# Seven eighths of the output projection planned inside the attention and RWKV stage, with one set of PSUM banks and a bias table written pair by pair

## The chip, the cores and the metric

The kernel runs on one core of a Trainium2 chip, in one launch. The core has a matrix engine (TensorE, PE in the profile, with its weight loads as PEld), two elementwise engines (VectorE, DVE; ScalarE, ACT), a slower general one (GpSimd, POOL) and a queue that issues transfers (SyncE, SP). Each works its own instructions in order, and semaphores hold one back until what it needs is done. The metric is device time in microseconds for one execution, the median of several runs. All times below are microseconds unless marked ns.

## What is computed

One layer over 512 tokens behind 16 meta tokens, width 1024, float32. Two branches of 16 heads read the same normalised input: attention over a window of 128 with a bias table and sinks, and an RWKV-7 recurrence. Gates merge them, an output projection follows, then a normalisation and an MLP. Cut to what matters:

```python
h = layer_norm(concat([meta, x]), ln0_g, ln0_b)          # 528 x 1024
proj = h @ w_in
q, k, v, zr, gate_att, gate_rwkv = split(proj)
att = sliding_window_attention(q, k, v, rel_bias, sinks)
rw = rwkv7_time_mix(zr, ...)                             # token shift, decay, state, group norm
merged = sigmoid(gate_att) * att + sigmoid(gate_rwkv) * rw
h = layer_norm(ALPHA * h + merged @ w_out, ln1_g, ln1_b)
ff = square(relu(h @ w_ff1)) @ w_ff2
out = layer_norm(ALPHA * h + ff, ln2_g, ln2_b)[meta:]
```

## The kernel before

**Products.** Every large product is made of three matmuls in a reduced float32 format: each factor is split in a high and a low part, and high by high, high by low and low by high are added up (`three`). A weight arrives as a raw tile of 128 x 1024 (`wraw`, two of them), ACT casts it to the high part (`whi`), DVE subtracts to get the low part (`wlo`); both are kept in halves of 512 columns. The normalised input lies transposed in `hhi` and `hlo` (128 x 8 x 528), one slice `k` of 128 channels for each of the eight steps of a contraction.

**The stage.** Heads are worked in eight pairs. For each pair `rwkv(j)` makes decay, key, receptance and value from five products, then scores within chunks of 64 tokens, the inverse of a triangular matrix for each chunk, folds, a chain of eight small products (`link`, one for each chunk), outputs, a group norm, and a tile `z`. The inverse goes through memory: blocks `Nd` are stored and gathered as `Nf`, POOL substitutes (`Xf`), the result is stored (`xtd`, `Xrd`) and gathered as `XB`, `X1` (`X` in the profile) and `XTm`. `attention(j)` makes queries, scores with a bias, softmax, the output and both gates. `merge(j)` gates and adds the two into `z` and stores it in DRAM (`md`).

**The order.** None of this is ordered as written. Each function records operations in a plan: `op(engine, cost, fn, r=, w=, new=)`, with an estimated cost, what is read and written, and which buffers are taken (`new`) from rings of tiles (`Ring`, `Buf`). `order` then places all operations by a list schedule at build time: for each engine the ready operation with the earliest due time goes next. Due times are counted back from the end of each pair, `SLOT` (58 us) times its number. A PE operation of another kind than the last (`mode`) is put back by `HYST`. A transfer's result is taken to be there a fixed lag after its issue, 2.3 us or a number beside it. What comes out is a fixed sequence for each engine; on the chip the semaphores wait for the data itself, whatever the plan thought.

**Memory.** PSUM has eight banks: three (`dn`) for the dense products and five (`pg`) for all else. Fourteen tiles (`e`) serve the elementwise work. The bias of the relative distance is made once: a table of 16 heads by 128 values is written to DRAM 128 times over (`tbd`, 1 MB), and each pair reads its part of it along a diagonal (`bias`).

**After the stage.** `merged(j)` loads `md[j]`, halves and splits it into `mhi` and `mlo`. `project_out(k, w, b)` adds slice `k` for block `b` of 128 tokens, both halves of the columns, six products; the first four `k` run over all blocks, the last four block by block. `norm_rows` normalises the input rows again for the residual, `first_norm(b)` adds the projection, normalises, transposes and splits into `h1hi` and `h1lo`; for the first two blocks it is issued between the products of later blocks (`NORMED`). The MLP follows (`up`, `project`), with its first three steps in two halves of tokens.

Of the kernel before, what the change touches and what calls it, by code (L numbers as in the profile page):

```python
# [77 lines left out]
HYST = 4000.0  # L78
# [6 lines left out]
NE = 14  # L85
# [8 lines left out]
SUBST = 1  # L94

# [52 lines left out]
class Buf:  # L148

    def __init__(self, ring):  # L150
# [21 lines left out]
class Plan:  # L172
# [3 lines left out]
    SAFE = SAFE  # L176

# [3 lines left out]
    def op(self, eng, cost, fn, r=(), w=(), new=(), mode="R", lag=None, after=(), part=None, port=0):  # L181
        o = Op(len(self.ops), eng, cost, fn, mode, self.LAG[eng] if lag is None else lag)
        o.part, o.port = part, port
# [29 lines left out]
    def stuck(self, cand, ready):  # L213
        out = []
        for e, c in cand.items():
            for _, o in sorted(c, key=lambda c: c[1].due)[:6]:
                out.append(f"{e} {o.fn.__qualname__.split('<locals>.')[-1]}:{o.fn.__code__.co_firstlineno} due {o.due / 1e3:.0f} new {[(len(b.ring.slots), len(b.ring.bufs), b.turn, b.ring.given) for b in o.new]}")
        held = {}
        for o in self.ops:
            if o.start is not None:  # L220
                for b in o.bufs:
                    if b.first is not None and b.first.start is not None and any(u.start is None for u in b.users):
                        held[b] = 1
        for b in held:
            if len(b.ring.bufs) > 30:
                out.append(f"held of {len(b.ring.bufs)}: {b.first.fn.__code__.co_firstlineno} due {b.first.due/1e3:.0f} left {[u.fn.__code__.co_firstlineno for u in b.users if u.start is None][:4]}")
        return "\n".join(out)

    def order(self, due, hyst, batch=0.0, hold=0.0, begin={}):
        for o in reversed(self.ops):  # L230
# [6 lines left out]
        port = 0.0  # L237
# [5 lines left out]
        wait = {o: len(o.deps) for o in self.ops}  # L243
        cand = {e: [] for e in self.LAG}
        left = {}
        for o in self.ops:
            for b in o.bufs:
                left[b] = len(b.users)
            if not o.deps:
                cand[o.eng].append((0.0, o))  # L250
        done, mode = [], "R"
        rings = {}

        def ready(t, o):
# [3 lines left out]
            for ring, bs in need.items():  # L258
                if len(ring.slots) < len(bs):
                    return None  # L260
                if ring.fifo and min(b.turn for b in bs) != ring.given:
                    return None
# [7 lines left out]
        while len(done) < len(self.ops):  # L270
# [21 lines left out]
            assert best is not None, "no operation can go on: " + self.stuck(cand, ready)  # L292
# [13 lines left out]
            for b in o.new:  # L306
                b.ring.slots.sort(key=lambda s: s[0])
                b.t = b.ring.slots.pop(0)[1]
                b.ring.given += 1
            o.start, o.end = t, t + cost  # L310
            if o.port:
# [7 lines left out]
            for s in o.after:  # L319
                wait[s] -= 1  # L320
                if wait[s] == 0:
                    cand[s.eng].append((max(self.seen(q, s.eng) for q in s.deps), s))
        return sorted(done, key=lambda o: (o.start, o.n))

@with_exitstack
def hybrid_layer_kernel(ctx: ExitStack, tc: tile.TileContext, I: dict, out: bass.AP):
# [4 lines left out]
    pps = ctx.enter_context(ExitStack())  # L331
    dn = pps.enter_context(tc.tile_pool(name="dn", bufs=3, space=PSUM))
    pg = pps.enter_context(tc.tile_pool(name="pg", bufs=5, space=PSUM))
# [51 lines left out]
    vps = pg.tile([P, 512], F32, name="vps", tag="g")  # L385
# [83 lines left out]
    tm = pg.tile([P, 512], F32, name="tm", tag="g")  # L469
# [16 lines left out]
    for k in range(KT):  # L486
        ks = slice(k * P, (k + 1) * P)
        if k % 2 == 0:
            tp = pg.tile([P, 512], F32, name="tp", tag="g")
        else:  # L490
            tp = pg.tile([P, 512], F32, name="tp", tag="g")
# [31 lines left out]
    rest = CONST.shape[1]  # L523
    nc.sync.dma_start(con[:, w0:rest], I["consts"][:, w0:rest])
# [30 lines left out]
    rdn = Ring([dn.tile([P, 512], F32, name="dn", tag="dn") for _ in range(3)], False)  # L555
# [1018 lines left out]
```

## Time and profile before

| | |
|---|---|
| median of 3 runs | 1019.02 us (1018.38 to 1019.12) |
| profiled execution | 1015.6 us, its span from first to last instruction 1013.8 us |
| mean granted PE clock | 0.964 |
| PE busy | 941.1 us |
| DVE, ACT, POOL busy | 578.8, 463.0, 127.8 us |
| transfers | 93.55 MB, mean 92 GB/s |

The profile is of one execution, taken by the hardware profiler. The page gives busy time of each engine, the span in 40 equal slices with busy tenths, and the costliest groups of instructions as `line engine operation out<-in shapes xcount | busy, mean ns | idle before, and what ended it`. Other views used below are: busy time by stretches of time, which ends with the granted clock (1.00 is full), the DMA share and GB/s; waits (who waited for whom: total, times, longest); the chain of work that ended last; and a timeline (start, duration, engine, line, operation, in brackets the idle time before it and what ended it). Durations of matmuls overlap, so distances between starts say more of their rate.

### The profile page before, as it was taken

Reading aid. Unit: us, or ns where it says so; the run is one execution under the profiler, and the core shown is the slowest. Engines: PE = TensorE matmul, PEld = TensorE weight load, DVE = VectorE, ACT = ScalarE, POOL = GpSimd, SP = SyncE. Lnnn points to the kernel's source line nnn. Section 1 sums busy time; section 2 is a strip of 40 time slices with the busy share of each in tenths; the row PEclk is TensorE's granted clock in tenths of the full one; section 3 lists DMA queues with packets and bytes.
Section 4 is the critical chain, followed back from the end, with each engine's and each line's share of the span. In section 5 each row is a group of like instructions: output and inputs, shape, how many; then the busy total and the mean of one; then the engine's idle time right before and its main releaser. Section 6 shows DMA issues by size and latency. Waiting matters only on the chain.

```text
span 1013.8 us, 18375 instructions
## 1 busy us (share of the span) xinstructions
PE 941.1 (93%) x7336; PEld 798.9 (79%) x7336; DVE 578.8 (57%) x1121; ACT 463.0 (46%) x1106; POOL 127.8 (13%) x372
## 2 busy tenths in 40 slices
PE   4996998998999989989999849999999999999996
PEld 3885896887978969879798638798888888888885
DVE  7653575674855847749467538766442334453336
ACT  5652646555565555464654523554431214343120
POOL 2030024041130230401304010000000000000001
PEclk9997999999999989999999959999999999999999
DMA  6345214043151340332403346123332323332232
GB/s 218 124 104 100 69 45 118 28 116 73 44 117 31 96 85 29 102 61 58 101 22 97 83 148 223 53 73 107 123 99 89 104 87 101 103 99 88 83 105 83
DMA packets 83311, 93.55 MB, mean 92 GB/s; under 512 B 54935, under 2 KB 61833, under 8 KB 83225
## 3 DMA queue, kind: packets, MB, share of 16 engines
q1 hardware_dynamic: 81728, 90.29, 32.0%
q10 hardware_dynamic: 1496, 2.08, 0.6%
q8 instruction: 57, 0.93, 0.4%
q14 instruction: 30, 0.24, 0.1%
HBM read 83.10 MB, written 9.26 MB: 91 GB/s over the span
## 4 chain that ended last, share of the span: by engine, by line
PE 63%; DMA 12%; POOL 9%; DVE 8%; issue 3%; ACT 3%; SPq 2%; DVEq 0%; POOLq 0%; ACTq 0%
PE dps L520 6%; PE dps L519 6%; PE dps L521 6%; PE acc L1389 6%; PE acc L1391 6%; PE acc L1390 6%; PE dn L519 4%; POOL ftmp L1015 4%; POOL Xf L1019 4%; PE dn L520 3%; PE dn L521 3%; DMA X<-Xrd 2%; DMA xtd<-Xf 2%; DMA Nd<-NT 2%; DMA Nf<-Nd 2%
## 5 line engine op out<-in xcount | busy, mean ns | idle before, releaser
L519 PE MATMUL dn<-hhi,whi 128*128 128x512 f32 (+3 forms) x640 | 218.4, 341 | 1.0 <-DVE e L721 0.6
L520 PE MATMUL dn<-hlo,whi 128*128 128x512 f32 (+3 forms) x640 | 205.2, 321 | 0.7 <-DVE hlo L502 0.7
L521 PE MATMUL dn<-hhi,wlo 128*128 128x512 f32 (+3 forms) x640 | 204.4, 319 | 0.0
L447 ACT CAST whi<-wraw 128x512 fp32r<-128x512 f32 x132 | 75.5, 619 | 223.9 <-PE acc L1391 105.6
L450 DVE TENSOR_TENSOR wlo<-wraw,whi 128x512 fp32r<-128x512 f32 x132 | 85.7, 688 | 152.0 <-ACT whi L447 151.7
L519 PEld LDWEIGHTS dn<-hhi,whi 128*128 128x128 f32 x640 | 122.7, 192 | 21.4 <-issue 9.5
L521 PEld LDWEIGHTS dn<-hhi,wlo 128*128 128x128 f32 x640 | 122.2, 191 | 8.3
L520 PEld LDWEIGHTS dn<-hlo,whi 128*128 128x128 f32 x640 | 122.6, 192 | 7.7 <-DVE hlo L502 1.1
L678 DVE TENSOR_TENSOR wlo<-wraw,whi 128x512 fp32r<-128x512 f32 x102 | 70.4, 698 | 52.0 <-ACT whi L676 51.4
L520 PE MATMUL dps<-h1lo,whi 128*128 128x512 f32 (+1 forms) x264 | 99.4, 377 | 0.0
L521 PE MATMUL dps<-h1hi,wlo 128*128 128x512 f32 (+1 forms) x264 | 99.3, 376 | 0.0
L519 PE MATMUL dps<-h1hi,whi 128*128 128x512 f32 (+1 forms) x264 | 99.2, 376 | 0.0
L1390 PE MATMUL acc<-wlo,fhi 128*128 128x512 f32 x240 | 93.4, 389 | 0.0
L1389 PE MATMUL acc<-whi,fhi 128*128 128x512 f32 x240 | 93.4, 389 | 0.0
L1391 PE MATMUL acc<-whi,flo 128*128 128x512 f32 x240 | 93.4, 389 | 0.0
L676 ACT CAST whi<-wraw 128x512 fp32r<-128x512 f32 x102 | 62.3, 617 | 53.8 <-PE dn L520 28.0
L415 POOL TENSOR_TENSOR rsf<-rsf,mhalf 128x1 f32<-128x1 f32 x8 | 6.3, 786 | 404.1 <-DVE rsf L414 362.2
L520 PEld LDWEIGHTS dps<-h1lo,whi 128*128 128x128 f32 x264 | 49.7, 188 | 9.2 <-DVE h1lo L1445 0.2
L521 PEld LDWEIGHTS dps<-h1hi,wlo 128*128 128x128 f32 x264 | 49.7, 188 | 9.1
L519 PEld LDWEIGHTS dps<-h1hi,whi 128*128 128x128 f32 x264 | 49.6, 188 | 9.0
L1391 PEld LDWEIGHTS acc<-whi,flo 128*128 128x128 f32 x240 | 45.0, 188 | 9.4
L1389 PEld LDWEIGHTS acc<-whi,fhi 128*128 128x128 f32 x240 | 45.0, 188 | 9.3
(273 smaller groups left out, 1635.2 us busy)
## 6 DMA issues: line engine op xcount, KB each, us to landing
wraw<-in_w_ff_dram SPq DMA_DIRECT2D x64, 512.0 KB, 3.6
wraw<-in_w_in_dram SPq DMA_DIRECT2D x52, 512.0 KB, 3.7
wraw<-in_w_out_dram SPq DMA_DIRECT2D x8, 512.0 KB, 3.4
xt<-in_x_dram SPq DMA_DIRECT2D x4, 512.0 KB, 7.4
Nd<-NT SPq DMA_DIRECT2D x16, 128.0 KB, 3.1
G<-in_consts_dram SPq DMA_DIRECT2D x16, 128.0 KB, 4.2
XB<-xtd SPq DMA_DIRECT2D x16, 128.0 KB, 4.2
md<-z SPq DMA_DIRECT2D x8, 256.0 KB, 2.6
```

The costliest lines, as they stand in the source:

```text
L447: act.copy(hi[:n, qs], raw[:n, qs])
L450: dve.tensor_tensor(lo[:n, qs], raw[:n, qs], hi[:n, qs].bitcast(F32), op=ALU.subtract)
L519: pe.matmul(ps, whi, xhi, start=first, stop=False)
L520: pe.matmul(ps, whi, xlo, start=False, stop=False)
L521: pe.matmul(ps, wlo, xhi, start=False, stop=last)
L676: AC(512, lambda hi=hi, qs=qs: act.copy(hi.t, raw.t[:, qs]), plain=True, r=[raw], w=[hi], new=[hi])
L678: f = lambda hi=hi, lo=lo, qs=qs, e=e: e.tensor_tensor(lo.t, raw.t[:, qs], hi.t.bitcast(F32), op=ALU.subtract)
L1015: sub(nj * nt, lambda s=s, nj=nj, nt=nt, tv=tv: se.tensor_tensor(tv(), Xf.t[:, 0:nj, s : s + 1].to_broadcast([NB, nj, nt]), Nf.t[:, s : s ...
L1019: sub(nj * nt, lambda s=s, nj=nj, tv=tv: se.tensor_tensor(Xf.t[:, 0:nj, s + 1 :], Xf.t[:, 0:nj, s + 1 :], tv(), op=ALU.add), r=tmps, w=[Xf])
L1389: pe.matmul(acc[b], xhi[:, k, bs], hi[:, ws], start=first, stop=False)
L1390: pe.matmul(acc[b], xhi[:, k, bs], lo[:, ws], start=False, stop=False)
L1391: pe.matmul(acc[b], xlo[:, k, bs], hi[:, ws], start=False, stop=last)
```

## The change

- The seven stored pairs are projected inside the plan. `merged(j)` becomes an operation that loads `md[j]` into an `e` buffer and writes it over `hhi` and `hlo`; the plan therefore lets it follow the last input product that reads the slice. `out_half(n)` takes half of the columns: it loads gains and biases, four residual rows, seven halves of `w_out`, and adds 7 x 4 units of three products into four banks, then adds the result to the residual. Pair 7 is projected after the stage, in six products for each block, and `first_norm` adds it.
- One set of eight banks, in two pools, serves the stage, the projection and the MLP.
- Of the fourteen `e` tiles, eight are halves of the residual rows' tiles; a residual row must get its own (`only`).
- Buffers that an evicting operation took are now taken by the product before it (`into`, longer `new` lists). Several operations read more than they need, which delays them in the plan.
- A transfer has a `wire` time; transfers queue behind one another in the plan, and each lands 1.8 us after its wire time.
- The bias table is written as 16 rows of 128 (`tbh`), and each pair writes its own 128 KB in DRAM and reads it back along the diagonal.
- The small meta products move from a bank shared with the norms to a later one (`meta0`).
- `HYST` falls from 4000 to 2500; the recurrence of each pair is due 20 us (`AHEAD`) before its pair. A plan that gets stuck is made anew with an order added (`jam`, `attempt`).

```diff
-HYST = 4000.0
+HYST = 2500.0
-NE = 14
+NE = 6
+AHEAD = 20000.0
...
+    LAND = 1800.0
...
+        if wire is not None:
+            o.lag = wire + self.LAND
...
+            if o.wire is not None:
+                queue = max(queue, o.end) + o.wire
+                o.lag = queue - o.end + self.LAND
...
-    dn = pps.enter_context(tc.tile_pool(name="dn", bufs=3, space=PSUM))
-    pg = pps.enter_context(tc.tile_pool(name="pg", bufs=5, space=PSUM))
+    pa = ctx.enter_context(tc.tile_pool(name="pa", bufs=1, space=PSUM, side="right"))
+    pb = ctx.enter_context(tc.tile_pool(name="pb", bufs=1, space=PSUM))
+    banks = [(q, f"acc{i}") for q in (pa, pb) for i in range(4)]
...
+    rest = [mg.tile([P, 2 * T], F32, name=f"res{b}") for b in range(4)]
     re_ = ring("e", at, [P, T], NE, fifo=False, keep=KEEPE)
+    re_.slots += [(0.0, row(b, n)) for b in range(4) for n in range(2)]
...
-                op("PE", 1393 if n == 512 else 6 * (13 + n / 2.4) - 12, seg, r=[hi, lo], w=[ps], new=[ps] if s == 0 else [])
+                op("PE", 1393 if n == 512 else 6 * (13 + n / 2.4) - 12, seg, r=[hi, lo, (bh, 2 * s), (bh, 2 * s + 1)], w=[ps], new=[ps] + (list(into) if t0 == spans[0][0] else []) if s == 0 else [])
...
-        op("SP", 100, lambda: nc.sync.dma_start(tbd, tbs.t[0:HEADS, 0, :].unsqueeze(1).to_broadcast([HEADS, P, P])), r=[tbs], w=[btb], lag=6000)
+        op("SP", 100, lambda: nc.sync.dma_start(tbh, tbs.t[0:HEADS, 0, :]), wire=100, r=[tbs], w=[btb])
...
+        op("SP", 100, lambda: nc.sync.dma_start(tbd.t, tbh[2 * j : 2 * j + 2].unsqueeze(1).to_broadcast([2, P, P])), wire=800, r=[btb], w=[tbd], new=[tbd])
...
-        op("SP", 100, lambda: nc.sync.dma_start(Nf.t, blocks(Nd.t, 0, [BSTEP, NB], [C, B], [1, B])), r=[Nd], w=[Nf], new=[Nf], lag=2500)
+        op("SP", 100, lambda: nc.sync.dma_start(Nf.t, blocks(Nd.t, 0, [BSTEP, NB], [C, B], [1, B])), wire=3300, r=[Nd], w=[Nf], new=[Nf])
...
-        op("PE", 630, inv1, r=[NT, X1], w=[up], new=[up], mode="Q")
+        op("PE", 630, inv1, r=[NT, X1, XB], w=[up], new=[up, U, U2, X2], mode="Q")
...
-            gin = [(G, ("F", e, c // 4)) for e in range(2)]
+            gin = [(G, ("F", e, i)) for e in range(2) for i in range(2)]
...
         due[last] = SLOT * (j + 1)
+        due[a["last"]] = SLOT * (j + 1) - AHEAD
...
+    def merged(j):
+        m = A[j]["z"]
+        if j < PAIRS - 1:
+            m = Buf(re_)
+            op("SP", 100, lambda: nc.sync.dma_start(m.t[:, :SEQ], md[j]), wire=950, r=[(bmd, j)], w=[m], new=[m])
+        AC(512, lambda: act.activation(hhi[:, j, NMETA:], m.t[:, :SEQ], AF.Copy, scale=0.5), r=[m], w=[(bh, j)])
+        DV(512, more=60, fn=lambda: dve.scalar_tensor_tensor(
+            hlo[:, j, NMETA:], m.t[:, :SEQ], 0.5, hhi[:, j, NMETA:].bitcast(F32), op0=ALU.mult, op1=ALU.subtract),
+           port=1, r=[m], w=[(bh, j)])
...
+        for k in range(PAIRS - 1):
+            (hi,), (lo,) = weights("w_out", k, [n])
+            for b in range(4):
+                def unit(k=k, b=b, hi=hi, lo=lo):
+                    project_out(acc[b].t, k, b, hi.t, lo.t, k == 0, k == PAIRS - 2)
+
+                op("PE", 681, unit, r=[hi, lo, (bh, k)], w=[acc[b]], new=[acc[b]] if k == 0 else [])
+        for b in range(4):
+            last = DV(512, more=60, fn=lambda b=b: dve.scalar_tensor_tensor(
+                res[b].t[:, :SEQ], res[b].t[:, :SEQ], ALPHA, acc[b].t, op0=ALU.mult, op1=ALU.add), r=[acc[b]], w=[res[b]])
+            due[last] = SLOT * PAIRS + 8000.0 * (n + 1)
+
+    def project_out(ps, k, b, hi, lo, first, last):
+        bs = slice(NMETA + b * P, NMETA + (b + 1) * P)
+        pe.matmul(ps, hhi[:, k, bs], hi, start=first, stop=False)
+        pe.matmul(ps, hhi[:, k, bs], lo, start=False, stop=False)
+        pe.matmul(ps, hlo[:, k, bs], hi, start=False, stop=last)
...
     for b in range(4):
-        for k in range(KT - WOL, KT):
-            project_out(k, wout[k - KT + WOL], b)
+        for n in range(2):
+            project_out(acc[b, n], PAIRS - 1, b, wlast[0][n].t, wlast[1][n].t, True, True)
         if 0 < b <= NORMED:
             first_norm(b - 1, pa, acc)
```

More of the change, by code (lines that the diff above doesn't have):

```diff
@@ L229, in order, with jam @@
-    def order(self, due, hyst, batch=0.0, hold=0.0, begin={}):
+    def jam(self, cand, extra):
+        for o in sorted((o for c in cand.values() for _, o in c if o.new), key=lambda o: (o.due, o.n)):
+            for ring in dict.fromkeys(b.ring for b in o.new):
+                late = [b.first for b in ring.bufs if b.first is not None and b.first.start is not None
+                        and any(u.start is None for u in b.users) and b.first.due > o.due]
+                late = [f for f in late if (o, f) not in extra]
+                if late and not ring.fifo:
+                    return o, max(late, key=lambda f: (f.due, f.n))
+        raise AssertionError("no operation can go on")
@@ new lines, in order @@
+    def order(self, due, hyst, batch=0.0, hold=0.0, begin={}):
+        extra, rings = {}, {}
+        for o in self.ops:
+            for b in o.bufs:
+                rings.setdefault(b.ring, list(b.ring.slots))
+        while True:
+            done, cand = self.attempt(due, hyst, batch, hold, begin, extra)
+            if len(done) == len(self.ops):
+                return sorted(done, key=lambda o: (o.start, o.n))
+            extra[self.jam(cand, extra)] = 1
+            for r, slots in rings.items():
+                r.slots, r.given = list(slots), 0
+            for o in self.ops:
+                o.start = o.end = None
+                if o.wire is not None:
+                    o.lag = o.wire + self.LAND
@@ L230, in order, with attempt @@
+    def attempt(self, due, hyst, batch, hold, begin, extra):
         for o in reversed(self.ops):
@@ L243, in order @@
         wait = {o: len(o.deps) for o in self.ops}
+        then = {}
+        for x, y in extra:
+            wait[y] += 1
+            then.setdefault(x, []).append(y)
         cand = {e: [] for e in self.LAG}
@@ L521, in three @@
         pe.matmul(ps, wlo, xhi, start=False, stop=last)
[L523 to L524 removed]
+    nc.sync.dma_start(con[:, w0:], I["consts"][:, w0:])
     sinks = cst.tile([P, HEADS], F32, name="sinks")
@@ L626, in hybrid_layer_kernel @@
     bzwa, bsg, blom, bk_, bv_, btb = (Buf(single(x)) for x in (zwa, sghi, lom, khi, vtok, None))
-    tbd = dr.tile([HEADS, P, P], F32, name="tbd")
+    rtbd = Ring([dr.tile([2, P, P], F32, name=f"tbd{i}") for i in range(2)])
+    bh, bmd = Buf(single(hhi)), Buf(single(None))
+    tbh = dr.tile([HEADS, P], F32, name="tbh")
     md = dr.tile([PAIRS, P, SEQ], F32, name="md")
@@ L666, in PO, with weights @@
         return op("POOL", cp(n), fn, **k)
-    def weights(name, i):
+    def weights(name, i, qs_=(0, 1)):
         raw = Buf(rraw)
-        op("SP", 100, lambda: nc.sync.dma_start(raw.t, I[name][i]), w=[raw], new=[raw], lag=4500)
+        part = slice(qs_[0] * 512, (qs_[-1] + 1) * 512)
+        op("SP", 100, lambda: nc.sync.dma_start(raw.t[:, part], I[name][i, :, part]), wire=950 * len(qs_), w=[raw], new=[raw])
         his, los = [], []
-        for q in range(2):
+        for q in qs_:
             hi, lo = Buf(rhi), Buf(rlo)
@@ new lines, in project_out @@
+    def project_out(ps, k, b, hi, lo, first, last):
[3 more added lines that the diff above has]
+        pe.matmul(ps, hlo[:, k, bs], hi, start=False, stop=last)
+    for j in range(PAIRS):
+        merged(j)
+    for n in range(2):
+        out_half(n)
+    wlast = weights("w_out", PAIRS - 1)
+    op("-", 0, lambda: None, r=kept + wlast[0] + wlast[1], after=list(plan.ops))
@@ L1502, in hybrid_layer_kernel @@
             if half == 0 and f in (6, 10):
-                row = rowvec(("ln1_g", "ln1_b")[f // 10], wst, "wraw")
+                gb_ = rowvec(("ln1_g", "ln1_b")[f // 10], wst, "wraw")
                 for b in range(4):
-                    dve.tensor_tensor(res[b], res[b], row, op=(ALU.mult, ALU.add)[f // 10])
+                    for n in range(2):
+                        dve.tensor_tensor(res[b][n], res[b][n], gb_[:, n * 512 : (n + 1) * 512], op=(ALU.mult, ALU.add)[f // 10])
         if half == 0:
```

293 lines of the change are left out of this document (126 added, 167 removed).

## The prediction

> **What bounds the kernel now.** I read the page first: the span, the busy shares, PE and its clock by slices.
>
> ```profile
> span 1013.8 us, 18375 instructions
> ...
> PE 941.1 (93%) x7336; PEld 798.9 (79%) x7336; DVE 578.8 (57%) x1121; ACT 463.0 (46%) x1106; POOL 127.8 (13%) x372
> ...
> PE   4996998998999989989999849999999999999996
> ...
> PEclk9997999999999989999999959999999999999999
> ```
>
> PE is the only engine near its limit, so a change can win only the time in which PE stands, or runs at a reduced clock. The digits show two holes: the fourth slice (76 to 101 us) and the twenty-fourth (583 to 608), both with the lowest clock too. So I asked for busy time by stretches: the first hole, six pairs between (first and last shown), the last pair, the output projection, the MLP. Columns: stretch, length, busy us of PE, weight load, DVE, ACT, POOL, then granted clock.
>
> ```profile
> 81.50:95.00 13.50, 6.26 (x29) 5.52 (x30) 2.14 (x6) 2.56 (x6) 0.54 (x3) 0.50 0.61 138
> 147.00:213.00 66.00, 62.44 (x647) 52.62 (x646) 44.01 (x94) 37.20 (x98) 16.17 (x42) 0.95 0.30 77
> ...
> 478.00:540.00 62.00, 59.75 (x627) 51.75 (x626) 40.44 (x87) 34.54 (x93) 10.94 (x40) 0.97 0.29 74
> 540.00:605.00 65.00, 46.30 (x496) 36.10 (x495) 32.34 (x69) 29.95 (x83) 15.14 (x35) 0.83 0.34 97
> 605.00:655.70 50.70, 49.12 (x217) 40.39 (x218) 37.68 (x57) 20.25 (x42) 1.67 (x3) 0.95 0.45 153
> 655.70:1013.80 358.10, 350.41 (x1618) 292.77 (x1616) 165.48 (x257) 113.49 (x211) 4.62 (x5) 0.99 0.30 96
> ```
>
> The last stretch is the MLP, 350 of 358 us busy and left as it is: 358 us follow whatever comes before. The waits of PE say who made the holes (total, times, longest):
>
> ```profile
> PE g L1041 <- DMA X<-Xrd: 18.1, 6, 3.3
> PE g L1113 <- DMA XTm<-xtd: 9.5, 1, 9.5
> ...
> PE o L1349 <- ACT mhi L1326: 8.4, 1, 8.4
> ...
> PE dn L519 <- DVE e L721: 0.6, 1, 0.6
> ```
>
> This gives a ledger of four losses. (a) Pair 0: 9.5 us behind XTm, and the 6.26 us of work between 81.5 and 95 ran at half clock, 3.1 lost: 12.6. (b) Pairs 1 to 6: 18.1 us in six waits for X; a clock of 0.95 to 0.97 over six such stretches is some 29 us at half, 19 of them the standing itself, so 10 us of work ran at half, 5 lost: 23. (c) Last pair: 65.0 - 46.3 = 18.7 us standing. In the slice from 583 to 608 PE is busy four tenths, 10 us, 3.4 of them after 605, so about 7 us ran at half, 3.5 lost: 22. (d) Output projection: 50.7 - 49.1 = 1.6 standing, and 2.5 lost to the clock (below): 4. Sum 62 us, a bound on what a better order can win.
>
> **The change part by part.** First the projection. The rows are the last scores of pair 7, the last input product, the fold that ends the hold of GR, the end of the chain, and the old projection from its first product to the first of the MLP.
>
> ```profile
> 538.89 1.20 PE L915 MATMUL g<-G,BK 64*128 64x128 f32 x16
> ...
> 567.25 0.40 PE L521 MATMUL dn<-hhi,wlo 128*128 128x512 f32 x1
> ...
> 578.01 2.06 PE L1096 MATMUL g<-GR,WT 64*128 64x128 f32 x32
> ...
> 599.50 0.69 DVE L1285 TENSOR_TENSOR z<-z,e 128x512 f32<-128x512 f32 x1
> ...
> 605.02 0.76 PE L1349 MATMUL o<-whi,mhi 128*128 128x512 f32 x1 [8.43 <-ACT mhi L1326]
> ...
> 610.27 0.49 PE L1349 MATMUL o<-whi,mhi 128*128 128x512 f32 x1
> ...
> 629.20 0.39 PE L1351 MATMUL o<-whi,mlo 128*128 128x512 f32 x1
> ...
> 655.58 0.36 PE L519 MATMUL dps<-h1hi,whi 128*128 128x256 f32 x1
> ```
>
> From 610.27 to 629.20 start 83 products after one another, 0.228 us each; the twelve before took 5.25 us, 0.44 each, so half clock cost 2.5. Seven of eight pairs are 168 products, 38.3 us, that move into the stage. They can start only when no input product still reads hhi, since the merged rows are written over it: 567 us in this order. Chain: from the scores at 538.9 to z at 600.2 pass 61 us. PE work beside it: 46.3 + 38.3 = 84.6 us. So the last pair becomes bound by PE instead of by its chain, with some 20 us of room for the chain to be late. I count 17 of the 22 us of (c) as won; 5 stay, because the projection's units are ordered by the plan, with a few waits for rows and weights. Breaking it into units of three between small products costs a refill at each change of kind, as after four transposes:
>
> ```profile
> 565.14 1.12 PE L1253 MATMUL g<-con,sb 128*128 128x128 f32 x4 [0.34 <-ACT sb L1239]
> 566.01 0.48 PE L519 MATMUL dn<-hhi,whi 128*128 128x512 f32 x1
> 566.33 0.39 PE L520 MATMUL dn<-hlo,whi 128*128 128x512 f32 x1
> ```
>
> The next product starts 0.32 later instead of 0.23. For 168 / 3 = 56 units that is at most 5 us; I take 3.
>
> Its feed: a half load of w_out or of md is 256 KB. The issues of the page bound it, a store of that size below and a load of twice the size above; cast and subtraction stand there too:
>
> ```profile
> L447 ACT CAST whi<-wraw 128x512 fp32r<-128x512 f32 x132 | 75.5, 619 | 223.9 <-PE acc L1391 105.6
> L450 DVE TENSOR_TENSOR wlo<-wraw,whi 128x512 fp32r<-128x512 f32 x132 | 85.7, 688 | 152.0 <-ACT whi L447 151.7
> ...
> wraw<-in_w_out_dram SPq DMA_DIRECT2D x8, 512.0 KB, 3.4
> ...
> md<-z SPq DMA_DIRECT2D x8, 256.0 KB, 2.6
> ```
>
> With cast (0.62) and subtraction (0.69) and some 0.3 of handing over, a raw buffer turns in 4.2 to 5.0 us, two of them give a half in 2.1 to 2.5, and twelve products use it in 2.7. It suffices, barely. The eight extra evictions on DVE (0.69 each by the subtraction, which has their shape) and the row normalisation in halves lie beside PE work: DVE is busy 44 of 66 us per pair. Without that cover they would cost 5.5 us.
>
> *What stays behind.* Pair 7 of the projection (24 products, 5.5 us) and the four normalisations. Before, each block had 24 products to hide the next block's normalisation; now six. The price is read from block 0 (its addition, its scaling, the next block's scaling, its last h1lo; then its transposes):
>
> ```profile
> 637.05 1.28 DVE L1425 SCALAR_TENSOR_TENSOR res<-res,o 128x512 f32<-128x512 f32 x2
> ...
> 641.16 0.81 DVE L1430 TENSOR_SCALAR res<-res,fmv,rsf 128x1024 f32<-128x1024 f32 x1 [0.74 <-POOL rsf L415]
> ...
> 645.47 0.81 DVE L1430 TENSOR_SCALAR res<-res,fmv,rsf 128x1024 f32<-128x1024 f32 x1 [0.68 <-POOL rsf L415]
> 646.20 1.32 DVE L1445 TENSOR_TENSOR h1lo<-h1f,h1hi 128x512 fp32r<-128x512 f32 x2
> ...
> 642.03 1.09 PE L1436 MATMUL tp<-con,res 128*128 128x128 f32 x8 [1.56 <-DVE res L1430]
> ```
>
> One block takes 10.5 us (637.05 to 647.5), each further one 4.3 on DVE. The MLP's first products need two blocks, 15 us, and beside these PE has 18 products (4.1) and 24 transposes (2.5): 8.4 us standing. Blocks 2 and 3 add about 1.5 of waiting, and the restart at half clock 2.5 as at 605. So 12.4 us stand where (d) had 4. Bounds: 8 if splitting and evicting fall well, 18 if the weight splits of the MLP come in between.
>
> On the clock, the Trainium skill ("TensorE: Matmul & The Clock Gate", What's actually happening) says that the clock halves after an idle window of about 3.4 us and returns after a busy one. By that rule the restart would cost 1.7 us, and the sum would be under 1 us better. The row at 605 says 2.5, and by the skill's rule, too, the new standing is long enough to lose the clock.
>
> *Bias table by pairs, and transfers charged.* The hole of pair 0 comes from one transfer: the 1 MB table takes 15.0 us, the small write behind it 10.2 against 2.4 in another pair.
>
> ```profile
> tbd<-bias SPq DMA_DIRECT2D x1, 1024.0 KB, 15.0
> ...
> 75.34 10.20 DMA xtd<-Xf
> ...
> 231.92 2.39 DMA xtd<-Xf
> 235.67 4.48 DMA X<-Xrd
> ```
>
> Pieces of 128 KB, and an order that knows of the queue, should win 10 of the 12.6. Each pair gets one more write on SP's queue, of under a tenth of the bytes that its weights bring; what is behind it there is the bias load, which now waits for it, and behind that the scores of attention, for which no row shows a wait on the table: nothing, and 2.6 us a pair (the store's row) if that cover were gone. In pairs 1 to 6 the product on X is placed before X lands. With the chain of three transfers charged, the plan puts input products there instead; these are the same work moved, so the wait itself is won. I take 16 of 23, the rest being new misplacements. Bounds: 0, if another late transfer takes its place, and 23.
>
> *One set of eight banks, buffers taken with the products, extra reads, HYST and AHEAD.* These change only the order that the plan writes; no instruction gains work, and the extra reads are no waits on the chip. Where a buffer is claimed by the product, a dense step waits in the plan and not on the engine. The row of 0.6 us says buffers were not short, so I take nothing, with -5 (banks freer) and +10 us as ends.
>
> **Sum** on the profiled execution: 10 + 16 + 17 + 4 - 12.4 - 3 = 31.6, say 31 us. The MLP starts at 624.5 instead of 655.6, the span is 983 and the time 1015.6 - 31 = 984.6. The median of the runs, 1019.0, lies 3.4 above the profiled execution, so I forecast 988.
>
> **Rivals.** *All is won:* a and b whole, the boundary 8: 12.6 + 23 + 20 + 4 - 8 - 3 = 49, so 970. For it: 20 us of room for the chain. Against: any static order has waits that it didn't foresee.
> *The middle keeps its waits* under another name: a and b give 5 instead of 26: 1009. For it: six waits of the same size show how such a plan errs. Against: they all have one cause, which is charged now.
> *The projection comes too late* (the change doesn't do what it says): the guard on hhi, or the feed, holds the units until the chain has ended; (c) gives 0: 1005. For it: feed 2.5 against 2.7. Against: 33 us lie between the last input product and z.
> *Slower: the chain becomes the pace.* NT and GR have one buffer; they are held from scores to the second fold, 538.9 to 580, 41 us of a period of 66. The charges make the planned transfers (fixed 1.8 each, 3.2 for the gathers) some 12 us longer than the rows above, and each of about ten small steps can be held up to 1.5 us: 65. From a hold of 66 on the period follows it. At 70, seven periods lose 28 us; c and a still give 27, the boundary takes 8.4 net, 3 refill: 1019 + 28 - 27 + 8 + 3 = 1031. Against it: AHEAD puts the chain first, and stretching to 65 only just reaches it.
>
> **How the numbers follow.** Forecast (972 to 1001) 0.60; all won 0.12; middle keeps its waits 0.08; projection late 0.06; slower 0.11; gains and losses cancelling, 0.03. The range 966 to 1011 holds the first four but for the edges. A difference under 0.2% (2 us) can't be told from none: faster 0.86, same 0.03, slower 0.11.
>
> **What would show it.** Right: no wait on XTm over 1 us; the X waits under 6 us in sum; output products between the links of pair 7, at full clock; z within 5 us of the last moved product; PE standing 8 to 12 us before the first MLP product, which starts near 625; the MLP still 358 us. Wrong: a period above 66 us in the pairs, waits of PE on `e` buffers or on w_out, or the moved products all behind z.

## The result and the profile after

The changed kernel takes 979.37 us (median of 4 runs, 976.9 to 980.4) against 1018.70 for the kernel before on the same chip: ratio 0.963, 95% interval 0.958 to 0.967. The profiled execution took 980.4 us, its span 978.6: 35.2 less than before. The forecast was 988 with a range of 966 to 1011, so the sign and the range were right, and the gain was 8 us larger than forecast (39 for 31).

The page of the changed kernel, the same lines as before:

```profile
span 978.6 us, 18391 instructions
...
PE 934.4 (95%) x7336; PEld 791.3 (81%) x7336; DVE 587.7 (60%) x1149; ACT 460.6 (47%) x1106; POOL 149.8 (15%) x372
...
PE   4999999999999999999998996899999999999996
...
PEclk9999999999999999999997998799999999999999
```

The hole in the fourth slice is gone. In place of the one at 583 to 608 us, where the last pair ended, there are two smaller ones: in slice 22 (514 to 538 us), inside the last pair, and in slices 25 and 26 (587 to 636), which now hold the boundary before the MLP. The busy time by stretches of the changed kernel, cut at its own events: pair 0, six periods (first and last shown), the last input products, the moved products, the boundary, the MLP:

```profile
60.00:100.00 40.00, 39.85 (x297) 36.31 (x295) 22.61 (x41) 24.37 (x56) 13.25 (x35) 1.00 0.50 134
...
147.00:213.00 66.00, 65.58 (x690) 55.69 (x689) 47.43 (x103) 38.29 (x100) 21.48 (x54) 1.00 0.32 86
...
478.00:523.60 45.60, 44.47 (x465) 36.76 (x463) 30.03 (x63) 22.96 (x63) 12.59 (x32) 1.00 0.31 84
523.60:545.25 21.65, 18.27 (x213) 13.71 (x212) 11.44 (x20) 11.81 (x30) 1.27 (x1) 0.68 0.47 130
545.25:593.66 48.41, 48.40 (x338) 39.15 (x330) 28.05 (x49) 13.42 (x30) 2.15 (x2) 1.00 0.32 104
593.66:617.08 23.42, 11.03 (x41) 8.11 (x41) 21.04 (x42) 11.37 (x26) 2.69 (x4) 0.75 0.31 103
617.08:978.60 361.52, 353.78 (x1624) 296.23 (x1624) 167.51 (x269) 114.87 (x214) 4.62 (x5) 0.99 0.30 95
```

This is the account in standing time of PE. Pair 0: 9.5 us became 0.2. The pairs up to the last scores: 18.8 (the six stretches from 147 to 540 us before) became 4.8 (the six from 147 to 523.6 here). The last pair: 18.7 became 3.4, all of it ahead of 545 us; the 48.4 us in which the moved products run between the steps of pair 7 have none. The boundary before the MLP: 1.6 became 12.4. With 1 us in the first 60 us that is 28.5 us less standing; the other 6.7 of the 35.2 are busy time (941.1 to 934.4 for the same 7336 instructions), which fits less work at half clock.

Who PE waits for now, where DMA X and DMA XTm stood before:

```profile
...
PE tp L1471 <- DVE res L1465: 7.5, 2, 3.9
...
PE o L1378 <- ACT hhi L1341: 3.4, 1, 3.4
...
PE g L1292 <- ACT sb L1278: 2.0, 1, 2.0
PE g L1304 <- ACT pall L1296: 1.7, 2, 1.4
```

No wait of the stage is on a transfer any more. The waits for `sb` and `pall` are the new hole at 523 us. Its timeline on PE: the last large product ahead of it, and the next one, 13 us later, which is the first of the last segments of an input product; then the end of the input products, and the first moved one. Between the first two rows stand the softmax of attention and other small steps, with the two waits.

```profile
523.22 0.40 PE L553 MATMUL g<-sghi,gwl 128*128 128x512 f32 x1
...
536.07 0.79 PE L551 MATMUL g<-hhi,whi 128*128 128x512 f32 x1
...
544.31 0.39 PE L553 MATMUL g<-hhi,wlo 128*128 128x512 f32 x1
...
545.25 0.51 PE L1378 MATMUL g<-whi,hhi 128*128 128x512 f32 x1
```

No instruction waits here for a buffer: the plan had put this product behind the softmax. Its weights had long been split. What it needed besides were tiles of the `e` ring, and the transfers show who had them. Five merged pairs were read back into such tiles as soon as they were stored, at 150.43, 212.57, 273.70, 335.38 and 396.34 us (first shown), and kept them until `hhi` could be written over, slice by slice (from 537.75 us on) behind this very product, which is the last to read it; two more tiles were filled at 506.50 and 506.98:

```profile
150.43 0.42 SPq L1340 DMA_DIRECT2D res<-md  x1
...
506.50 0.43 SPq L1340 DMA_DIRECT2D e<-md  x1
506.98 0.43 SPq L1353 DMA_DIRECT2D e<-in_rows_dram  x1
```

That is a step that the prediction had priced at nothing, and the experiments test it.

### The profile page after: what moved, and what is told of

Read it like the earlier page. It is cut to its first block, busy times and chain, and to the rows that moved or that the text cites. A ratio compares the mean times of both kernels' runs of the same rounds, so it can differ in the third digit from the quotient of the medians.

```text
span 978.6 us, 18391 instructions
## 1 busy us (share of the span) xinstructions
PE 934.4 (95%) x7336; PEld 791.3 (81%) x7336; DVE 587.7 (60%) x1149; ACT 460.6 (47%) x1106; POOL 149.8 (15%) x372
## 4 chain that ended last, share of the span: by engine, by line
PE 71%; DVE 13%; ACT 6%; POOL 4%; DMA 3%; issue 2%; SPq 0%; DVEq 0%; POOLq 0%; ACTq 0%
PE g L551 6%; PE dps L551 6%; PE dps L552 6%; PE acc L1426 6%; PE acc L1425 6%; PE acc L1427 6%; PE dps L553 6%; PE g L552 5%; PE g L553 5%; DMA wraw<-in_w_in_dram 2%; DVE G L962 2%; PE g L1125 2%; PE g L1112 1%; PE g L952 1%; POOL ftmp L1044 1%
## 5 line engine op out<-in xcount | busy, mean ns | idle before, releaser
L551 PE MATMUL g<-hhi,whi 128*128 128x512 f32 (+3 forms) x640 | 213.4, 333 | 0.1
L552 PE MATMUL g<-hlo,whi 128*128 128x512 f32 (+3 forms) x640 | 204.7, 320 | 1.1 <-DVE hlo L534 1.1
L553 PE MATMUL g<-hhi,wlo 128*128 128x512 f32 (+3 forms) x640 | 204.0, 319 | 0.0
L482 ACT CAST whi<-wraw 128x512 fp32r<-128x512 f32 x124 | 70.9, 620 | 210.1 <-PE acc L1427 105.6
L485 DVE TENSOR_TENSOR wlo<-wraw,whi 128x512 fp32r<-128x512 f32 x124 | 80.3, 687 | 142.9 <-ACT whi L482 142.8
L551 PEld LDWEIGHTS g<-hhi,whi 128*128 128x128 f32 x640 | 121.0, 189 | 16.8 <-issue 6.0
L553 PEld LDWEIGHTS g<-hhi,wlo 128*128 128x128 f32 x640 | 121.1, 189 | 8.7
L552 PEld LDWEIGHTS g<-hlo,whi 128*128 128x128 f32 x640 | 121.2, 189 | 8.1 <-DVE hlo L534 1.5
L715 DVE TENSOR_TENSOR wlo<-wraw,whi 128x512 fp32r<-128x512 f32 x118 | 81.2, 697 | 42.7 <-ACT whi L713 41.8
L713 ACT CAST whi<-wraw 128x512 fp32r<-128x512 f32 x118 | 71.4, 615 | 51.6 <-PE g L552 21.4
L1044 POOL TENSOR_TENSOR ftmp<-Xf,Nf 66x15 f32<-66x15 f32 (+7 forms) x120 | 45.7, 381 | 204.4 <-DMA Nf<-Nd 196.4
```

Of the source, the lines that this page charges most:

```text
L482: act.copy(hi[:n, qs], raw[:n, qs])
L485: dve.tensor_tensor(lo[:n, qs], raw[:n, qs], hi[:n, qs].bitcast(F32), op=ALU.subtract)
L551: pe.matmul(ps, whi, xhi, start=first, stop=False)
L552: pe.matmul(ps, whi, xlo, start=False, stop=False)
L553: pe.matmul(ps, wlo, xhi, start=False, stop=last)
L713: AC(512, lambda hi=hi, qs=qs: act.copy(hi.t, raw.t[:, qs]), plain=True, r=[raw], w=[hi], new=[hi])
```

## The experiments

Every ratio is to runs of the kernel before on the same chip, whose medians were 1016.9 to 1020.7 us. The changed kernel's ratio is 0.963 (0.958 to 0.967).

| run | us | ratio, 95% interval |
|---|---|---|
| moved products behind pair 7 | 991.74 | 0.973, 0.967 to 0.980 |
| transfers not charged | 994.87 | 0.976, 0.969 to 0.984 |
| 1 MB written again | 988.51 | 0.969, 0.963 to 0.975 |
| before, one lag 6000 | 1008.06 | 0.988, 0.982 to 0.994 |
| rows loaded late | 998.64 | 0.979, 0.976 to 0.981 |
| no holding | 971.87 | 0.953, 0.950 to 0.955 |
| both | 987.21 | 0.968, 0.965 to 0.970 |
| both, pair 6 kept back | 988.80 | 0.970, 0.967 to 0.973 |
| all row loads gated | 984.27 | 0.965, 0.962 to 0.968 |
| gated, no holding | 986.06 | 0.966, 0.963 to 0.970 |
| gated, no holding, pair 6 kept back | 990.26 | 0.970, 0.967 to 0.973 |
| no holding, only the last loads gated | 964.87 | 0.946, 0.943 to 0.949 |

### The moved products without their cover

The theory was that the moved products pay because they fill the chain of pair 7. The run makes them wait for its end.

```diff
-  ... new=[acc[b]] if k == 0 else [])
+  ... new=[acc[b]] if k == 0 else [], after=[A[PAIRS - 1]["z_op"]])
```

> The changed kernel, but the plan lets no unit of the seven moved pairs start before z of pair 7 is complete. All else stays. Theory (the projection pays because it fills PE while the last chain runs): the chain runs alone again, about 1.5 us a link instead of 3, z comes some 10 us earlier than in the changed kernel, and then 192 products (44 us) follow; the MLP starts 17 to 25 us later, 996 to 1004 us in all. Rival (the filling only stretches the chain by as much as it hides): within 5 us of 979.

It took 991.74, 11 us more by the ratio and 12 by the median, between the two expectations. Its stretches, and the end of its chain and of its moved products:

```profile
545.00:560.00 15.00, 9.46 (x116) 8.23 (x116) 12.41 (x22) 2.97 (x8) 0.00 (x0) 0.77 0.24 80
560.00:580.00 20.00, 14.42 (x76) 11.53 (x77) 7.44 (x14) 4.41 (x10) 2.92 (x2) 0.66 0.25 79
```

```profile
574.96 0.69 DVE L1324 TENSOR_TENSOR z<-z,e 128x512 f32<-128x512 f32 x1
...
611.31 0.40 PE L1381 MATMUL g<-whi,hlo 128*128 128x512 f32 x1
611.55 0.39 PE L1379 MATMUL o<-whi,hhi 128*128 128x512 f32 x1
```

The same two places in the changed kernel:

```profile
593.26 0.39 PE L1380 MATMUL g<-whi,hlo 128*128 128x512 f32 x1
...
595.69 0.69 DVE L1324 TENSOR_TENSOR z<-z,e 128x512 f32<-128x512 f32 x1
597.09 0.50 PE L1378 MATMUL o<-whi,hhi 128*128 128x512 f32 x1 [3.44 <-ACT hhi L1341]
```

From 545 to 580 PE stands 11.1 us at a reduced clock: the old hole. The last moved product starts at 611.31 in place of 593.26, so the cover is worth 18.0 us there, as the theory had it. But 7 us of that are given back behind it: with the chain to itself z is done 20.7 us sooner, pair 7's products follow the moved ones without the stand of 3.4 us and without its half clock, and the MLP starts 11.0 later (628.07 for 617.08). So the run showed a second thing that I had not looked for: in the changed kernel the moved products hold the chain up by so much that its end comes last.

### The two repairs of transfers

In the first of these runs the planned transfers have their old fixed lags (4500 for weights, 2500 and 2600 for the stores and gathers of the inverse) and no queue. In the second the transfers are charged, but the 1 MB table is also written, to a place that nobody reads.

```diff
-        o.part, o.port, o.wire = part, port, wire
-        if wire is not None:
-            o.lag = wire + self.LAND
+        o.part, o.port, o.wire = part, port, None
```

```diff
+        tbig = dr.tile([HEADS, P, P], F32, name="tbig")
+        op("SP", 100, lambda: nc.sync.dma_start(tbig, tbs.t[0:HEADS, 0, :].unsqueeze(1).to_broadcast([HEADS, P, P])), wire=100, r=[tbs])
```

> The changed kernel, with the old fixed lags of the transfers in the plan (4.5 us for weights, 2.5 for the gathers, 2.3 else) and no queue in it. Theory (the charge removes the waits of pairs 1 to 6): PE waits for X again, six or seven times some 3 us, with work at half clock behind them, 15 to 23 us more, 994 to 1002 us. Rival (the eight free banks and the buffers taken with the products did it): no wait for X above 1 us, within 3 us of 979.

> The changed kernel, with the old 1 MB table written beside the small one, to a place that nobody reads, charged in the plan as a small write. Theory (the one transfer made the hole of pair 0): the write of the inverse behind it takes 8 to 10 us again, PE stands 6 to 10 us in pair 0 and loses 2 to 3 more at half clock: 987 to 992 us. Rival (the hole came from what the plan had left to do in pair 0, which the new order cures): PE stands under 3 us, within 3 us of 979.

Uncharged it took 994.87, 14 us more by the ratio and 15.5 by the medians, as the theory said, but not by six waits for X. The waits of PE:

```profile
PE g L549 <- DVE sb L1239: 6.5, 3, 5.8
PE g L1068 <- DMA X<-Xrd: 6.4, 2, 3.5
PE g L1146 <- ACT SVm L1141: 4.7, 5, 1.4
```

X costs 6.4 us in two waits; as much goes to an input product that waits on DVE's work in the softmax (`sb`), 5.8 us of it in pair 0, where PE stands 7.5 us between 60 and 100 us. So this run doesn't price the charge in pairs 1 to 6 alone: the wrong lags lose here in many places. With the 1 MB back it took 988.51, 9 us more by the medians and 10.3 by the spans, inside the theory. In the chain of what ended last, by time, the hole is there again with another wait at its end:

```profile
75.96 11.00 DMA tbd<-tbh
...
87.47 4.24 DMA wraw<-in_w_in_dram
91.79 0.63 ACT whi L713
92.46 0.59 PE g L551
```

A write of 128 KB took 11.00 us behind the 1 MB. The bias load waits for it, and with the bias load the queue: the weights behind it are issued at 87.47 us, where the changed kernel issues the same load at 78.77, and PE waited 8.0 us for them. The load itself took no longer, 4.24 us for 4.19. So the repair of pair 0 is worth 9 to 10 us by this run.

### The middle pairs by one number

In the kernel before, alone, the gather of `X1` is taken to land after 6000 instead of 2500.

```diff
-  nc.sync.dma_start(X1.t, ...), r=[Xrd], w=[X1], new=[X1], lag=2500)
+  nc.sync.dma_start(X1.t, ...), r=[Xrd], w=[X1], new=[X1], lag=6000)
```

> The kernel before, with one number changed: the lag that the plan gives the gather of X, 6000 ns instead of 2500. Theory (a misjudged landing is all of the loss in pairs 1 to 6, and needs no new banks or buffers): waits of PE for X fall from 18.1 to under 6 us, the time by 12 to 20, 999 to 1007 us; the hole of pair 0 stays. Rival (the wait passes on to the next step of the inverse): the waits of PE for X, XB and U together stay above 14 us, within 4 us of 1019.

It took 1008.06, 9 us less by the medians and 12 by the ratio: about half of the 23 us that the prediction gave to these waits, and at or just under the lower edge of the theory. PE waits for X nowhere any more. A wait for the next gather takes a part of their place, 10.8 us in pair 0 (9.5 before) and 5.8 in the others:

```profile
PE g L1113 <- DMA XTm<-xtd: 16.6, 8, 10.8
```

The stretches show where the rest went:

```profile
213.00:279.00 66.00, 65.20 (x686) 56.28 (x688) 46.57 (x102) 38.53 (x101) 17.61 (x45) 1.00 0.30 81
...
540.00:567.00 27.00, 22.66 (x301) 16.89 (x299) 14.40 (x30) 14.11 (x47) 8.24 (x22) 0.87 0.31 87
567.00:605.00 38.00, 21.33 (x114) 17.14 (x115) 14.58 (x26) 8.41 (x18) 2.91 (x2) 0.55 0.35 118
```

From 213 us on the pairs in the middle run as in the changed kernel, 65.2 of 66 at full clock; the stretch before, from 147 to 213, keeps a wait of 3.2 us for XTm and a clock of 0.95. The last pair now stands 21 us of 65 (18.7 before) and runs at a clock of 0.68 (0.83 before): products come earlier, its chain does not, and a part of the gain is given back there. So the parts of the change are not independent. That the changed kernel keeps what the charges win because the moved products fill the end is the likely reading; no run shows it by itself.

### The hole at 523 us, first attempts

Two edits, alone and together, and a third on top. *Rows late* lets the loads of merged pairs, of the norm's gains and biases and of the residual rows start only behind the last eight products that claim a tile. *No holding* ends, for the last pair, the rule that small PE steps are held up to 1.5 us to be issued in batches. *Pair 6 kept back* projects pairs 6 and 7 after the stage.

```diff
-  op("SP", ..., w=[r], new=[r])
+  op("SP", ..., w=[r], new=[r], after=claims[-PAIRS:])
```

```diff
-                        if work < batch and t0 - first < hold:
+                        if work < batch and t0 - first < (hold if t0 < TAIL else 0.0):
```

```diff
+            project_out(acc[b, n], PAIRS - 2, b, wsix[0][n].t, wsix[1][n].t, True, False)
...
-            project_out(acc[b, n], PAIRS - 1, b, wlast[0][n].t, wlast[1][n].t, True, True)
+            project_out(acc[b, n], PAIRS - 1, b, wlast[0][n].t, wlast[1][n].t, False, True)
```

> The changed kernel with one order forbidden: the loads of the merged pairs, the first norm's rows and the residual rows into e buffers may be issued only after the last eight dense tiles have taken theirs. Nothing is left out of the computation. Theory (claims cost 10 us in the last pair: the attention gate's product is held because the row loads issued at 506 to 512 us have taken the e buffers): PE stands under 1 us in place of 3.4 between 523 and 545 us and runs there at full clock, the moved products' weights and buffers still come in time, and the time falls by 5 to 10 us to 969 to 975. Rival (the last pair's chain sets the end, and the product of the gate is not on it): the hole closes, its 7 us open again between the links, and the time stays at 977 to 982. Second rival (late rows starve the moved products): PE waits on e or w_out tiles after 545 us, 982 to 990.

> The changed kernel with one constant of the planner altered for the last pair alone: from 520 us of plan time on, TensorE's small steps are no longer held back up to 1.5 us to be issued in batches. Nothing is left out. Theory (in the last pair the links, 3.0 us apart where they were 1.5 before, wait behind products that are put ahead of them, and z comes 3.4 us after the last moved product for that reason): the links come closer, z is ready while moved products still run, the 3.4 us wait for pair 7's hhi goes, 975 to 977. Rival (the chain and the products need the same PE time whatever their order, and what the links gain is lost in changes between small and large products): 978 to 982.

> Both alterations together: rows loaded late, and no holding of small steps in the last pair. Theory (two separate losses): the gains add, 966 to 973. Rival (both are the same slack, the end of pair 7's chain): no better than the better of the two alone, within 2 us of it.

> Both alterations, and in addition the products of pair 6 with w_out kept behind the stage beside those of pair 7: 24 products of 0.23 us, 5.4 us of TensorE, run where TensorE stood 3.4 us waiting for pair 7's hhi. Nothing is left out. Theory (the boundary is a sum: 3.4 us for hhi, then 8 to 9 us of norms behind the products): the 3.4 us are filled and the stage is 5.4 us shorter, so it is 2 to 4 us better than the run with both alterations. Rival (the last pair is bound by its chain, so taking products out of it opens gaps between links): no gain or up to 3 us worse than the run with both alterations.

Rows late took 998.64: 19 us slower than the changed kernel, which none of its three expectations allowed. The cause isn't in the last pair. In this kernel (first row) and in the changed one (second), the last score products of pair 7 start at

```profile
L956 PE MATMUL g<-G,BK x256: 272/272/374, 50.2 to 509.8; 64*128 64x128 f32 x128
```

```profile
L952 PE MATMUL g<-G,BK x256: 272/272/373, 50.2 to 494.1; 64*128 64x128 f32 x128
```

so 15.7 us are lost before the stretch under test. The early loads of merged pairs, from 150 us on, were held back too; so the plan of the pairs came out otherwise, and, it happens, slower. The run doesn't test the hole. Both edits together have the same flaw and so has the run with pair 6 kept back, which was no better than it (988.80 for 987.21).

No holding took 971.87, 7.5 us faster by the medians and 1.0% by the ratios, whose intervals don't touch; that is more than its theory (975 to 977). The links of pair 7, in the changed kernel and in this run (first two of seven each; of this run also the addition that completes z and the first product of pair 7):

```profile
564.88 0.38 PE L1186 MATMUL g<-Z,G 128*128 128x128 f32 x2
567.88 0.38 PE L1186 MATMUL g<-Z,G 128*128 128x128 f32 x2
```

```profile
554.33 0.38 PE L1187 MATMUL g<-Z,G 128*128 128x128 f32 x2
555.94 0.45 PE L1187 MATMUL g<-Z,G 128*128 128x128 f32 x2
...
574.51 0.69 DVE L1325 TENSOR_TENSOR z<-z,e 128x512 f32<-128x512 f32 x1
...
591.07 0.39 PE L1379 MATMUL o<-whi,hhi 128*128 128x512 f32 x1
```

The links come 1.1 to 2.1 us apart in place of 3.0, z is done 21 us earlier, and pair 7's products follow the moved ones without a wait. In the changed kernel four units of three products stand between two links. PE has work all the while, so nothing seems to be lost, until the end of the chain comes after the last moved product.

### The hole alone

The next three gave the loads of merged pairs and of the norm's gains and biases an earliest time in the plan (522 us) in place of an order.

```diff
-  op("SP", ..., wire=950, r=[(bmd, j)], w=[m], new=[m])
+  op("SP", ..., wire=950, r=[(bmd, j)], w=[m], new=[m], nb=ROWNB)
```

> The loads of the merged pairs and of the first norm's rows get an earliest issue time in the plan, 522 us, in place of an order behind the dense tiles; the residual rows are left as they were, and everything before the last pair keeps its place. Nothing is left out. The run with the order set it for all pairs in effect: its pairs 2 to 6 ran at 0.84 to 0.90 of the clock for a third of each period, so it did not test the hole alone. Theory (the row loads took the e buffers, and the gate's product waited for one): the gate's four segments of product come about 11 us earlier, the 3.4 us hole and the half clock behind it near 523 to 545 us are gone, and the time is 968 to 975. Rival (chain of the last pair sets the end): the hole goes, the links stay 3 us apart, 977 to 982.

> The same, with small steps not held back from 520 us of plan time on, which alone gave 971.9. Theory (two separate losses: the hole of 7 us, and the wait for hhi of pair 7): 963 to 968. Rival (once the links come early, PE has products for the whole of the last pair and the hole was only moved work): 970 to 974. A third: the links come so early that nothing small is left to run beside the moved products, and nothing is lost by it, 966 to 971, with moved products alone in the last 20 us of the stage.

> The same as the run before it, and the 24 products of pair 6 kept behind the stage too. With the links early, z of pair 7 should be ready while moved products still run, so nothing has to be filled while hhi is made; what is left of the boundary is DVE's and ACT's norm behind the last products of each block. Theory (the boundary is bounded by DVE's norms, which begin when the first block's products end): the stage is 5.4 us shorter, the first block is complete 4 to 5 us later after the stage, and the time stays within 2 us of the run before. Rival (the norm of the first block hides behind products of later blocks, whose number doubles): 3 to 5 us better.

They took 984.27, 986.06 and 990.26. My expectation that everything before the last pair would keep its place was wrong again: these loads too are the ones of 150 to 396 us, and in the first of the three runs the last scores start at 506.3. That run shows what the early loads are good for:

```profile
541.33 0.40 PE L554 MATMUL g<-hhi,wlo 128*128 128x512 f32 x1
...
559.31 0.77 PE L1379 MATMUL g<-whi,hhi 128*128 128x512 f32 x1
```

```profile
548.28 9.87 SPq L1341 DMA_DIRECT2D e<-md  x7
```

All seven merged pairs are read at 548 to 558 us, and the first moved product starts 18 us after the last input product, not 0.9 us. The hole had only moved. And keeping pair 6 back gave 990.26 for 986.06, 4 us more, with intervals that overlap, and by no means the 3 to 5 us gain of its rival.

So the last run leaves the early loads as they are. It is the run with no holding, and gates only those of the loads that its plan issued after 480 us; pairs 0 to 6 keep their plan.

```diff
+                for o in self.ops:
+                    o.nb = o.nb if o.start > 480000.0 else 0.0
```

> The run with no holding of small steps in the last pair (971.9), and one thing more: of the loads of merged pairs and of the first norm's rows, those that its plan issues after 480 us get an earliest issue time of 522 us. Up to 495 us of the plan nothing else moves, so pairs 0 to 6 must run as they do there; the earlier runs with late row loads had moved every pair. Nothing is left out. Theory (the gate's product was late because the row loads held e buffers, and that costs about 7 us of TensorE by itself): the product comes 11 us earlier in the plan, the stretch from 520 to 530 us is at 0.95 or more of the clock with no stand over 1 us, and the time is 963 to 968. Rival (the product only changes its place: TensorE then runs out of large products sooner, between the last input product and the first moved one or at the end of the stage): 969 to 974. A larger time than 976 would mean that late rows hold the moved products or the residual back.

It took 964.87, inside the theory and below the rival; the interval (0.943 to 0.949) lies under that of the run it builds on (0.950 to 0.955). The stretch from 500 to 545 us, first without and then with the gate:

```profile
500.00:545.00 45.00, 39.99 (x396) 30.64 (x397) 27.21 (x57) 28.77 (x77) 13.72 (x33) 0.92 0.44 121
```

```profile
500.00:545.00 45.00, 44.49 (x408) 35.78 (x407) 26.21 (x56) 28.11 (x75) 14.54 (x33) 1.00 0.50 141
```

PE stands 0.5 us in place of 5.0, at full clock in place of 0.92, and the timeline has the last input product and the first moved one close together, 16 us earlier than in the changed kernel:

```profile
528.00 0.40 PE L561 MATMUL g<-hhi,wlo 128*128 128x512 f32 x1
...
528.93 0.39 PE L1386 MATMUL g<-whi,hhi 128*128 128x512 f32 x1
```

The two plans, as the code of the two kernels writes them, show the cause too: they are the same, operation for operation, until the first of the gated loads takes its tile at 495.9 us of plan time. Without the gate no tile then stays free, and the product, whose inputs had been ready since 475.7, stands at 520.1; with the gate it stands at 505.4. So the last late loads took the tiles that kept the product back, and with the rest equal this costs 7.0 us by the medians, 6.6 by the ratios. This was measured with no holding; in the changed kernel itself it wasn't separated. This version is 14.5 us faster than the changed kernel and 55 faster than the one before.

Claims of buffers at the evictions as before, the two sets of banks, and the old `HYST` and `AHEAD` were not tried one by one in the changed kernel, so their own share stays open.

## Why the prediction came out as it did

**Bias table by pairs: 10 us forecast, right.** Standing in pair 0 fell by 9.4, and writing the 1 MB again cost 9 to 10. The reason held too: a small transfer behind it took 11.0 us.

**Transfers charged: 16 of 23 forecast, too little.** The waits for X and XTm are gone, and standing in these pairs fell by 14 of some 19 us; the clock, 0.95 to 0.97 before, is at 1.00 in five of the six stretches. That is 18 or more of the 23. I had kept 7 back for new misplacements, and few came. What I didn't foresee is that the gain hangs on the last pair: in the kernel before, without the moved products, a part of it was given back there (the run with one lag).

**Moved products: 17 of 22 forecast for the last pair.** Where they run, the whole 22 is won: 48.40 of 48.41 us busy at full clock. The guard on `hhi` and the feed, the rival, cost nothing: the first moved product starts 0.9 us after the last input product. The run that puts them behind the chain prices their cover at 18.0 us at the last moved product; 7 of these are lost again behind it, as the chain ends later for their sake. Of the 3 us for refills 1.3 were paid: large products follow a small step 14 times in this stretch, not 56, each time with the next one 0.31 to 0.35 behind instead of 0.23.

**Buffers taken with the products: nothing forecast, with bounds of -5 and +10. This is the step that failed.** "The row of 0.6 us says buffers were not short, so I take nothing." They were hardly short before; in the changed kernel five merged pairs and the rows of the norm live in the same fourteen tiles, and a claim by the product turns a lack of tiles into an order that no semaphore shows. So the sign that I had named, waits of PE on `e` buffers, could not appear. The hole at 523 us stands 3.4 us and drags PE at half clock to 540. Its price is 7.0 us by the last pair of runs, inside the bounds. It is also why the last pair's net gain is near the 17 after all, and that is luck: 22 won, 7 given back ahead of it.

**The boundary before the MLP: 12.4 us forecast, 17 to 18 measured.** PE stands 12.4 us from 593.66 to 617.08, but 12.4 was to include the restart. Beside it the 24 products of pair 7 start over 7.0 us (597.09 to the last at 604.04) in place of 5.2 at 0.228 each, and the MLP takes 361.5 where it took 358.1. The excess comes from the late z and not from the norms. In the run with no holding, where z is early, the boundary from the first product of pair 7 to the MLP is

```profile
591.07:607.57 16.50, 8.91 (x42) 6.68 (x40) 16.13 (x32) 10.86 (x25) 1.12 (x2) 0.85 0.30 96
```

PE stands 7.6 us in it, and the MLP takes 362.4, 4.3 more than before: 11.9 together, near the forecast. So the sum for the norms was right. What it left out was that z comes 2.7 us after the last moved product has ended; the prediction had allowed up to 5 and priced it at nothing.

**The rule of holding small steps: weighed only as a danger to the chain's pace**, in the slower rival, and at nothing for the end of pair 7. There it cost 7.5 us, most of them the excess of the boundary above. The slower rival, the chain as the pace of every pair, did not occur: the stretches of 66 us are full.

**The sum.** By the measured terms it is 10 + 18 + 22 + 4 - 17.5 - 7 - 1.3 = 28.2 us of the span, where 31.6 was forecast and 35.2 measured. Of the other 7.0, some 3.6 can be named: by its stretches pair 0 won the whole 12.5 (9.4 of standing and 3.1 at half clock) and not 10, and PE stands 1.1 us less in the first 60 us. The rest, 3.4 us, I can't assign: the half clock of the kernel before was only estimated. The closeness of the forecast thus owes something to errors of both signs.

## What to carry to other kernels

- When work is moved into a static plan to fill an engine, ask what its inputs will occupy while they wait. Tiles read back 140 to 390 us early made no wait on a transfer, but they and the last loads together left no tile for a product at the end. Reading all of them late left 18 us without moved work. What helped was to delay the last few alone.
- A hole whose only waits are short and on small steps can be a large product that the plan put too late. Look which large product comes next, and what it needed other than its data.
- Batching small steps pays while the chain has slack. In the last round the chain's end is the end of the stage, and the same rule delays it.

## What the runs showed of the hardware

Two things. First, a short stand can cost much more than its own length. Behind the 3.4 us of standing in the hole at 523 us the granted clock of the changed kernel was 0.50 from 528 to 540 us, although PE counted as busy in nearly all of it; until 536 that was small matmuls with 64 to 128 columns, and full clock came back only after 4 us of large products:

```profile
530.00:532.00 2.00, 2.00 (x13) 1.63 (x11) 0.69 (x1) 0.45 (x2) 0.00 (x0) 0.50 0.00 0
...
538.00:540.00 2.00, 2.00 (x6) 1.59 (x5) 1.43 (x3) 1.01 (x2) 0.00 (x0) 0.50 0.71 186
540.00:542.00 2.00, 2.00 (x70) 1.44 (x68) 1.30 (x3) 1.47 (x4) 0.00 (x0) 0.91 0.84 247
```

The Trainium skill ("TensorE: Matmul & The Clock Gate", What's actually happening) says that some 3.4 us of sustained activity bring the clock back. The large products come near it, with 4.0 us; the 8 us of small ones before them, busy by the profile, did not bring it back. But in the run with no holding, behind the same two waits (2.0 and 1.4 us), the clock was back at 531 us, 7 us after the first of the same small steps and before any large product, so how the gate counts such matmuls stays open.

Second, a write of 128 KB issued while 1 MB is being written took 11.0 us. The queue's next transfer needed it, and so the weight load behind that, which did not, was issued 8.7 us later than in the changed kernel: the delay is passed on to transfers that have nothing to do with the table.
